# A hybrid encoder step in fp32: weight sums of the channel stage by accumulating DMAs, and smaller state-space edits

## The chip, the cores and the metric

The kernel runs as one program on 1 core of one Trainium2 chip. The metric is device time in microseconds (us), the median of 3 runs. Six things work side by side in a core: TensorE (PE) multiplies, its weight loads (PEld) run beside the products, VectorE (DVE) and ScalarE (ACT) do elementwise work, GpSimd (POOL) and SyncE (SP) issue transfers, and DMA engines move the data. Each engine executes its own queue in order; semaphores connect them.

## The reference, cut to what matters

One layer is applied to 512 prompt rows and 128 sample rows (8 x 16), 640 in all. The mixing sub-layer comes first, the channel sub-layer behind it:

```
def encoder_layer(x, c, ...):
    u = rms_norm(x, g_pre_mix) * (1 + sc1) + sh1          # sc1, sh1 from silu(c) @ w_ada
    proj = u @ w_in                                       # -> z, xbc, dt_raw, p, gates
    ...                                                   # conv over xbc -> xs, bm, cm
    dt = softplus(dt_raw + dt_bias)
    y, h_final = ssd_chunked(xs, dt, a, bm, cm, h0)       # decay = exp(min(a_cs_l - a_cs_s, causal))
    y = y + xs * d_skip
    ...                                                   # norm, w_ssd_out, pooling branch, gates, w_o
    x = x + gt1 * rms_norm(mix, g_post_mix)
    v = rms_norm(x, g_pre_mlp) * (1 + sc2) + sh2
    hdn = jnp.square(jax.nn.relu(v @ w_up))               # 1024 -> 4096
    x = x + gt2 * rms_norm(hdn @ w_down, g_post_mlp)      # 4096 -> 1024
```

## The kernel before

**Precision.** Most products of fp32 data are made of three products of a reduced type: a matrix is split into a high half (ACT casts it) and a low half (DVE subtracts the cast from the original), and PE makes high x high, high x low and low x high. `split` (L132, L133) does this for weights: `wh`/`wl` are rings of four buffers, and every fifth split goes to the one buffer `wxh`/`wxl`.

**Prologue.** `ada_cols` makes the normalized input `uu` of two of eight row blocks and splits it; `dt_part` (L390 to L396) multiplies the dt weights with both halves in plain fp32 products, 80 instructions in all. `wpl`, the weight of the pooling branch, is loaded into room that the prologue's tiles leave.

**State space.** Eight groups, five blocks of 128 rows each: 40 calls of `common`. It reads the running sum `acs` back as rows (`ab`), subtracts each row's own sum by adding `nacs` and clips at zero in four DVE instructions (L711), takes one exponential on ACT (L712) and multiplies by `cb` (L713). `skip` (L720) adds D times x to the output from PSUM `py` in two DVE instructions a block.

**Channel sub-layer.** The 4096 hidden columns are cut in eight chunks e of 512. Each chunk has an up stage, two pairs (e,0) and (e,1) of 256 columns, and a down stage (`down`, L1219 for the products `pd`, L1237 for the sums into `acc`), which runs one chunk behind. A pair cuts its 1024 x 256 weight tile `wu` into four blocks (i,j), i the column half and j the row half, and its rows v in halves likewise; seven block products replace eight (84 instructions of 320 columns). For that it needs sums of weight blocks, made in the one buffer `S` by four DVE additions of 128 x 512:

```
first():   z = (2,1) + (2,2)        L1146       x0 = split of columns 0:128
           s = z + (1,1)            L1147       x1 = split of the two sums
second():  S[1] = s + (1,2)         L1154       x2 = split of the two sums
           S[0] = (1,1) + (2,1)     L1155       x3 = split of (2,2)
```

`run` makes the products (L1168): `pq` is a bank pair with the parts A_ and B_, `pr` the bank C_. The parts are emptied into `p1`, `u2`, `u3`, `q5` and the hidden tiles `f1`, `f2`; `put_hid` splits these (L1086, L1087). `t_blocks` makes the sums of v (t1 to t4, split into `TH`, `TL` and `AH`) from a copy of v which `make_v` wrote to DRAM (`v_d`, ten writes of 256 KB on POOL's queue). Chunk 0 is made without blocks before, beside the end of the mixing sub-layer; then come t_blocks, the down stage of chunk 0, and the pairs from (1,0) on. The next pair's `load` and `first` run inside `run` of the one ahead or inside `down`, at the row block t = 3.

**Order.** A scheduler sets each engine's order from the program's order and priorities; the high-priority parts are the splits and the sums. All loads of this stage are on SP's queue; POOL issues nothing there.

## Time and profile before

| what | value |
|---|---|
| median of 3 runs | 1381.33 us (1377.14 to 1384.82) |
| the profiled execution, its time | 1377.68 us |
| its span in the trace | 1375.9 us |
| PE busy | 1331.1 us (97%) |
| DVE busy | 918.0 us (67%) |
| ACT busy | 538.6 us (39%) |
| POOL busy | 90.8 us (7%) |
| DMA, mean | 140 GB/s |

How to read it: busy time is what an engine executes, and the span is the profiled execution from its first instruction to its last. An engine at 97% leaves little idle time to remove; the others wait for it. The stages lie about so: prologue to 90 us, input projection and state space to 627, the mixing output and v to 960, chunks 1 to 7 from 985 to the end.

### The profile page before, as it was taken

What the parts mean: (1) busy time and instruction counts of PE and PEld (TensorE: products, weight loads), DVE (VectorE), ACT (ScalarE), POOL (GpSimd) and SP (SyncE); (2) the same over time, 40 slices, a digit from 0 to 9 for tenths busy, and PEclk for the clock granted to TensorE, in tenths of its full rate; (3) what the DMA queues carried; (4) which work ended last, traced back from release to release, by engine and by line L of the source; (5) the groups of instructions that cost most, each with busy time, mean ns of one, the idle gap of its engine ahead of it and who ended that gap; (6) DMA issues with size and microseconds to landing.
All of it is one profiled execution on the core that took longest, in us unless ns stands there. A gap on an engine that the chain in (4) does not pass through costs nothing.

```text
span 1375.9 us, 22421 instructions
## 1 busy us (share of the span) xinstructions
PE 1331.1 (97%) x9008; PEld 1194.5 (87%) x9008; DVE 918.0 (67%) x1900; ACT 538.6 (39%) x961; POOL 90.8 (7%) x153
## 2 busy tenths in 40 slices
PE   4999999999999999999998999999989999999997
PEld 3999998878888889889898999788888988888886
DVE  4775668777776879687557332587575856757675
ACT  4443435444434454553434221355442422423331
POOL 0010010101201020102100000011000000000000
PEclk9999999999999999999999999999999999999999
DMA  9743523565546553435368533645122302122151
GB/s 295 224 102 119 167 88 111 154 218 184 164 149 219 179 181 87 131 104 172 111 206 268 193 111 119 214 153 184 32 82 72 123 31 92 67 88 92 62 199 46
DMA packets 134928, 192.26 MB, mean 140 GB/s; under 512 B 8541, under 2 KB 104877, under 8 KB 132776
## 3 DMA queue, kind: packets, MB, share of 16 engines
q1 hardware_dynamic: 124808, 161.27, 36.8%
q0 software_dynamic: 10016, 29.56, 6.9%
q8 instruction: 71, 1.16, 0.4%
q14 instruction: 33, 0.27, 0.1%
HBM read 159.20 MB, written 31.60 MB: 139 GB/s over the span
## 4 chain that ended last, share of the span: by engine, by line
PE 84%; DVE 5%; issue 4%; DMA 4%; ACT 2%; SPq 0%; POOL 0%; DVEq 0%; ACTq 0%; POOLq 0%
PE pd L1219 16%; PE px L161 16%; PE pz L161 8%; PE pso L161 8%; PE pq L1168 8%; PE pga L161 4%; PE pr L1168 3%; PE pp L161 3%; PE po L984 3%; PE py L725 2%; PE sp L745 1%; PE hTp L778 1%; PE ada L300 1%; PE yo L783 1%; PE tp L698 1%
## 5 line engine op out<-in xcount | busy, mean ns | idle before, releaser
L161 PE MATMUL px<-AH,wh 128*128 128x256 f32 (+1 forms) x512 | 119.1, 314 | 0.0
L161 PE MATMUL px<-AH,wl 128*128 128x256 f32 (+1 forms) x512 | 118.5, 310 | 0.0
L161 PE MATMUL px<-AL,wh 128*128 128x256 f32 (+1 forms) x512 | 118.0, 310 | 0.0
L161 PEld LDWEIGHTS px<-AH,wh 128*128 128x128 f32 x512 | 91.5, 188 | 7.8 <-issue 4.4
L161 PEld LDWEIGHTS px<-AL,wh 128*128 128x128 f32 x512 | 93.2, 188 | 0.5 <-issue 0.5
L161 PEld LDWEIGHTS px<-AH,wl 128*128 128x128 f32 x512 | 93.1, 188 | 0.5 <-issue 0.5
L1237 DVE TENSOR_TENSOR acc<-acc,pd 128x512 f32<-128x512 f32 (+1 forms) x61 | 41.1, 676 | 75.2 <-PE pd L1219 75.1
L1219 PE MATMUL pd<-wh,hh 128*128 128x512 f32 (+1 forms) x223 | 87.2, 394 | 1.9 <-ACT wh L132 1.7
L1219 PE MATMUL pd<-wl,hh 128*128 128x512 f32 (+1 forms) x223 | 87.9, 394 | 0.6 <-DVE wl L133 0.6
L1219 PE MATMUL pd<-wh,hl 128*128 128x512 f32 (+1 forms) x223 | 87.2, 393 | 0.0
L638 DVE SCALAR_TENSOR_TENSOR ac<-rw,colw,ac 128x640 f32<-128x640 f32 x96 | 84.4, 879 | 1.2 <-ACT ac L636 0.9
L161 PE MATMUL pz<-AH,wh 128*128 128x256 f32 (+1 forms) x256 | 62.1, 318 | 0.0
L161 PE MATMUL pz<-AH,wl 128*128 128x256 f32 (+1 forms) x256 | 61.6, 316 | 0.0
L161 PE MATMUL pz<-AL,wh 128*128 128x256 f32 (+1 forms) x256 | 61.5, 316 | 0.0
L161 PE MATMUL pso<-ynh,wh 128*128 128x256 f32 (+1 forms) x256 | 58.4, 309 | 2.6 <-ACT tgb L587 2.6
L132 ACT CAST wh<-S 128x1024 fp32r<-128x1024 f32 x22 | 23.1, 1048 | 95.2 <-DVE acc L1237 39.4
L161 PE MATMUL pso<-ynl,wh 128*128 128x256 f32 (+1 forms) x256 | 58.3, 309 | 0.0
L161 PE MATMUL pso<-ynh,wl 128*128 128x256 f32 (+1 forms) x256 | 58.2, 309 | 0.0
L1219 PEld LDWEIGHTS pd<-wh,hh 128*128 128x128 f32 x223 | 41.7, 188 | 12.6 <-ACT wh L132 2.7
L161 PEld LDWEIGHTS pz<-AH,wh 128*128 128x128 f32 x256 | 45.7, 188 | 6.1 <-issue 4.3
L1219 PEld LDWEIGHTS pd<-wl,hh 128*128 128x128 f32 x223 | 41.9, 188 | 10.2 <-DVE wl L133 1.5
L1219 PEld LDWEIGHTS pd<-wh,hl 128*128 128x128 f32 x223 | 41.9, 188 | 9.7 <-DVE hl L1087 0.3
(483 smaller groups left out, 3677.5 us busy)
## 6 DMA issues: line engine op xcount, KB each, us to landing
wada<-in_w_ada_dram SPq DMA_DIRECT2D x24, 1024.0 KB
wu<-in_w_up_dram SPq DMA_DIRECT2D x16, 1024.0 KB
wd<-in_w_down_dram SPq DMA_DIRECT2D x16, 1024.0 KB
ab<-acs_d SPq DMA_DIRECT2D x40, 256.0 KB
wxs<-in_w_in_dram SPq DMA_DIRECT2D x8, 1024.0 KB
wbc<-in_w_in_dram SPq DMA_DIRECT2D x16, 512.0 KB
wz<-in_w_in_dram SPq DMA_DIRECT2D x8, 1024.0 KB
h<-in_state_ssm_dram SPq DMA_DIRECT2D x16, 512.0 KB
```

Source lines behind the costliest of these rows:

```text
L132: S.copy(h, src)
L161: T.matmul(reg(ps, g), ww[:, kw, :], aa[g][:, ka, :], start=first and i == 0 and j == 0, stop=last and i == n - 1 and j == 2)
L300: T.matmul(st["ps"][32 * cg:32 * cg + 32, 0:n], cT[:, k, :], st["w"][:, k % kr, n * cg:n * (cg + 1)], start=k == 0, stop=k == 7, tile_posi ...
L638: V.scalar_tensor_tensor(a3, rw[:, :, k:k + 16], colw[:, 32 * k + ci:32 * k + ci + 1], a3, ALU.mult, ALU.add)
L698: T.transpose(tp[:, 128 * i:128 * (i + 1)], xc[:, i, ts], ident)
L725: T.matmul(py[64 * j:64 * (j + 1), 128 * qq:128 * (qq + 1)], xr[:, 2 * qq + j, :], M[:, 2 * qq + j, :], start=True, stop=stop)
L745: T.matmul(sp[:, 0:256], bt, xrd, start=True, stop=True)
L778: T.transpose(pt[:, 128 * b:128 * (b + 1)], st["h0"][qq][:, 4 * hb + b, :], ident)
L984: T.matmul(ps[:, HC[half]], aa[:, k, :], ww[:, HC[half]], start=k == 0 and j == 0, stop=k == 7 and j == 2)
L1168: T.matmul(dst, ww[:, k, :], aa[:, k, :], start=start and k == 0 and j == 0, stop=stop and k == 3 and j == 2, skip_group_check=True)
L1219: T.matmul(ps, aa[:, k, :], ww[:, cols], start=first and k == 0 and j == 0, stop=last and k == n - 1 and j == 2)
L1237: V.tensor_tensor(acc[t][:, hc], acc[t][:, hc], ps, ALU.add)
```

## The change

It has five parts.

1. `dt_part` multiplies the dt weights with `uu` itself instead of its two halves: 40 instructions instead of 80. The tile `uu` is kept in `uus`.
2. In `common` the clip is made first, in one DVE instruction on 128 x 512: min(ab, pacs), where `pacs` is the running sum with its own sign. Then four ACT instructions take the exponential with `nacs` as bias. D times x is written into `yb` by two ACT copies per group (`start`), and `skip` is one DVE addition of 128 x 256 per block.
3. `t_blocks` loads v into `acc_f` and works in place; the split of t3 is given back as `t3_late`. Pair (1,0) is made without block sums (`plain`, 96 products), ahead of t3's split; pair (1,1) follows, then the down stage of chunk 0, then chunks 2 to 7 as before. `run` uses `f1` and `f2` in place of `u2`, `u3`, `q5`.
4. Of the four sums of a pair, DVE makes one: z1 = s0 + (1,2) (L1164 in the changed kernel), at high priority.
5. The other three are made by DMAs into two buffers `Sa` and `Sb`, one of each. For Sa, SP loads block (2,1) into both halves; POOL adds (2,2) to both and then (1,1) to s0. For Sb, SP loads (1,1) into z0 and POOL adds (2,1). `sums_a` of the next pair is issued behind this pair's `first`, `sums_b` behind its `second`.

The diff, cut to these parts:

```diff
     def dt_part(b, k):
-        for j, aa in enumerate((uh, ul)):
-            for t in range(4):
-                T.matmul(dps[32 * t:32 * t + 32, 0:128], wdt[:, k, :], tok_cols(aa, t)[:, k, :].bitcast(F32),
-                         start=k == 0 and j == 0, stop=k == 7 and j == 1, tile_position=(0, 32 * t))
-            T.matmul(dps4[32 * b:32 * b + 32, 0:128], wdt[:, k, :], tok_cols(aa, 4)[:, k, :].bitcast(F32),
-                     start=k == 2 * b and j == 0, stop=k == 2 * b + 1 and j == 1, tile_position=(0, 32 * b))
+        uu = uus[b]
+        for t in range(4):
+            T.matmul(dps[32 * t:32 * t + 32, 0:128], wdt[:, k, :], uu[:, k - 2 * b, 128 * t:128 * (t + 1)],
+                     start=k == 0, stop=k == 7, tile_position=(0, 32 * t))
+        T.matmul(dps4[32 * b:32 * b + 32, 0:128], wdt[:, k, :], uu[:, k - 2 * b, 512:640],
+                 start=k == 2 * b, stop=k == 2 * b + 1, tile_position=(0, 32 * b))
...
         S.activation(nacs, acs_ps, AF.Copy, scale=-1.0)
+        S.copy(pacs, acs_ps)
...
+            V.tensor_tensor(M, ab, pacs[:, t, hs].unsqueeze(2).broadcast_to([128, 4, 128]), ALU.min)
             for hh in range(4):
-                V.tensor_scalar(M[:, hh, :], ab[:, hh, :], nacs[:, t, 4 * g + hh:4 * g + hh + 1], 0.0, ALU.add, ALU.min)
-            S.activation(M, M, AF.Exp)
+                S.activation(M[:, hh, :], M[:, hh, :], AF.Exp, bias=nacs[:, t, 4 * g + hh:4 * g + hh + 1])
...
-        def skip(qq, ts, py):
-            V.scalar_tensor_tensor(st["yb"][:, qq, ts], st["xc"][:, qq, ts], dsk[:, 2 * g + qq:2 * g + qq + 1],
-                                   py[:, 128 * qq:128 * (qq + 1)], ALU.mult, ALU.add)
+        def skip(ts, py):
+            yt = st["yb"][:, :, ts]
+            V.tensor_tensor(yt, yt, py[:, 0:256].rearrange("p (q n) -> p q n", q=2), ALU.add)
 
...
         def start():
+            for qq in range(2):
+                S.activation(st["yb"][:, qq, :], st["xc"][:, qq, :], AF.Copy, scale=dsk[:, 2 * g + qq:2 * g + qq + 1])
...
     def t_blocks():
-        vs = [F.tile([128, 4, 640], F32R, tag="h" + c, name=f"vs{c}", bufs=2).bitcast(F32) for c in "hl"]
-        for i, v in enumerate(vs):
-            Y.dma_start(v, v_d[4 * i:4 * i + 4].rearrange("k p n -> p k n"))
-        f11, f12, f21, f22 = vs[0][:, :, 0:HT], vs[0][:, :, HT:640], vs[1][:, :, 0:HT], vs[1][:, :, HT:640]
-        c1, c2, c3 = (acc_f[:, 1280 * i:1280 * (i + 1)].rearrange("p (k n) -> p k n", k=4) for i in (1, 2, 3))
+        vs = acc_f.rearrange("p (k n) -> p k n", k=8)
+        for i in range(2):
+            Y.dma_start(vs[:, 4 * i:4 * i + 4], v_d[4 * i:4 * i + 4].rearrange("k p n -> p k n"))
+        f11, f12, f21, f22 = vs[:, 0:4, 0:HT], vs[:, 0:4, HT:640], vs[:, 4:8, 0:HT], vs[:, 4:8, HT:640]
 
         def st(dst, src):
             S.copy(dst[0], src)
             V.tensor_tensor(dst[1], src, dst[0].bitcast(F32), ALU.subtract)
 
-        V.tensor_tensor(c1, f11, f12, ALU.subtract)
-        V.scalar_tensor_tensor(c2, c1, -1.0, f22, ALU.mult, ALU.subtract)
-        st(t1, c1)
-        st(t2, c2)
-        V.scalar_tensor_tensor(c3, c2, -1.0, f21, ALU.mult, ALU.subtract)
-        st(t4, c3)
-        V.tensor_tensor(c1, f22, f12, ALU.subtract)
-        st(t3, c1)
+        V.tensor_tensor(f11, f11, f12, ALU.subtract)
+        V.tensor_tensor(f12, f22, f12, ALU.subtract)
+        V.scalar_tensor_tensor(f22, f11, -1.0, f22, ALU.mult, ALU.subtract)
+        st(t1, f11)
+        st(t2, f22)
+        V.scalar_tensor_tensor(f21, f22, -1.0, f21, ALU.mult, ALU.subtract)
+        st(t4, f21)
+        return lambda: st(t3, f12)
 
...
+        def sums_a(self):
+            self.s = s = Q.tile([128, 2, 4, 128], F32, tag="Sa", name=f"Sa{self.n}", bufs=1)
+            Y.dma_start(s[:, 0], self.src(2, 1))
+            Y.dma_start(s[:, 1], self.src(2, 1))
+            G.dma_start(s[:, 0], self.src(2, 2), accum_op=ALU.add)
+            G.dma_start(s[:, 1], self.src(2, 2), accum_op=ALU.add)
+            G.dma_start(s[:, 0], self.src(1, 1), accum_op=ALU.add)
+
+        def sums_b(self):
+            self.z = z = Q.tile([128, 2, 4, 128], F32, tag="Sb", name=f"Sb{self.n}", bufs=1)
+            Y.dma_start(z[:, 0], self.src(1, 1))
+            G.dma_start(z[:, 0], self.src(2, 1), accum_op=ALU.add)
+
...
         def first(self):
-            r = self.r
-            self.s = sm = Q.tile([128, 2, 4, 128], F32, tag="S", name=f"S{self.n}", bufs=1)
+            self.x0 = split(self.r[:, :, 0:128], *KF)
             with tc.high_priority():
-                V.tensor_tensor(sm[:, 1], self.blk(2, 1), self.blk(2, 2), ALU.add)
-                V.tensor_tensor(sm[:, 0], sm[:, 1], self.blk(1, 1), ALU.add)
-            self.x0 = split(r[:, :, 0:128], *KF)
-            self.x1 = split(sm, *KH)
+                V.tensor_tensor(self.z[:, 1], self.s[:, 0], self.blk(1, 2), ALU.add)
+            self.x1 = split(self.s, *KH)
 
         def second(self):
-            sm = self.s
-            with tc.high_priority():
-                V.tensor_tensor(sm[:, 1], sm[:, 0], self.blk(1, 2), ALU.add)
-                V.tensor_tensor(sm[:, 0], self.blk(1, 1), self.blk(2, 1), ALU.add)
-            self.x2 = split(sm, *KH)
+            self.x2 = split(self.z, *KH)
             self.x3 = split(self.blk(2, 2), "p (k f) -> p k f", dict(k=4), n=512)
+
...
+        def plain(self):
+            for i in range(2):
+                ps = big(f"pq{self.n}{i}")
+                w = split_k(self.r, i)
+                for k in range(8):
+                    for j, (ww, aa) in enumerate(((w[0], vh), (w[0], vl), (w[1], vh))):
+                        for g in range(2):
+                            T.matmul(ps[:, 512 * g:512 * g + HT], ww[:, k, :], aa[g][:, k, :], start=k == 0 and j == 0, stop=k == 7 and j == 2)
+                f = rl_tile(self.e, 2 * self.fp + i)
+                for g in range(2):
+                    S.activation(f[:, HT * g:HT * (g + 1)], ps[:, 512 * g:512 * g + HT], AF.Relu)
+                V.tensor_tensor(f, f, f, ALU.mult)
+                put_hid(self.e, 2 * self.fp + i, f)
 
...
-            p1, u2, u3, q5 = tl("p1"), tl("u2"), tl("u3"), tl("q5")
+            p1 = tl("p1")
             f1, f2 = rl_tile(e, 2 * self.fp), rl_tile(e, 2 * self.fp + 1)
             prod(A_, a11, b11, True, True)
             S.copy(p1, A_)
             prod(B_, sl(self.x1, 0), t2, True, True)
-            V.tensor_tensor(u2, p1, B_, ALU.add)
+            V.tensor_tensor(f1[:, HT:640], p1, B_, ALU.add)
             prod(C_, sl(self.x1, 1), t1, True, True)
-            S.copy(q5, C_)
+            S.copy(f2[:, 0:HT], C_)
             if nxt:
                 nxt()
             prod(A_, a12, b21, False, True)
             S.copy(f1[:, 0:HT], A_)
             prod(B_, sl(self.x2, 0), t3, False, True)
-            V.tensor_tensor(u3, p1, B_, ALU.add)
+            V.tensor_tensor(f2[:, HT:640], p1, B_, ALU.add)
+            V.tensor_tensor(f2[:, HT:640], f2[:, HT:640], f2[:, 0:HT], ALU.add)
             prod(C_, sl(self.x2, 1), b22, False, True)
-            V.tensor_tensor(f1[:, HT:640], u2, C_, ALU.add)
+            V.tensor_tensor(f1[:, HT:640], f1[:, HT:640], C_, ALU.add)
             V.scalar_tensor_tensor(f1, f1, 0.0, f1, ALU.max, ALU.mult)
             put_hid(e, 2 * self.fp, f1)
             prod(B_, self.x3, t4, False, True)
-            V.tensor_tensor(f2[:, HT:640], u3, q5, ALU.add)
             V.tensor_tensor(f2[:, 0:HT], p1, B_, ALU.add)
...
     def begin(p):
-        p.load()
         p.first()
-
-    def up(e, after, late):
+        if NX[p]:
+            NX[p].sums_a()
+
+    def run(p, after, late):
+        p.second()
+        if NX[p]:
+            NX[p].sums_b()
+        p.run(nxt=after, late=late)
+
+    up0()
+    hid[1] = hid_tiles(1)
+    P[0].load()
+    t3_late = t_blocks()
+    P[1].sums_a()
+    P[1].sums_b()
+    P[0].plain()
+    t3_late()
+    P[1].load()
+    begin(P[1])
+    w = []
+    run(P[1], lambda: w_rows(0, [], 0, w), lambda: w_rows(0, [], 1, w))
+    P[2].load()
+    down((0,), [w], nxt=lambda: begin(P[2]))
+    for e in range(2, 8):
+        w = []
         hid[e] = hid_tiles(e)
         pa, pb = pairs[e, 0], pairs[e, 1]
-        pa.second()
-        pa.run(nxt=lambda: begin(pb), late=pb.second)
-        pb.run(nxt=after, late=late)
-
-    up0()
-    w0 = w_rows(0, [], 1, w_rows(0, [], 0, []))
-    t_blocks()
-    down((0,), [w0], nxt=lambda: begin(pairs[1, 0]))
-    up(1, lambda: begin(pairs[2, 0]), None)
-    for e in range(2, 8):
-        w = []
-        up(e, lambda: w_rows(e - 1, [], 0, w), lambda: w_rows(e - 1, [], 1, w))
+        pb.load()
+        run(pa, lambda: begin(pb), None)
+        run(pb, lambda: w_rows(e - 1, [], 0, w), lambda: w_rows(e - 1, [], 1, w))
         if e < 7:
-            down((e - 1,), [w], nxt=lambda: begin(pairs[e + 1, 0]))
+            pc = pairs[e + 1, 0]
+            pc.load()
+            down((e - 1,), [w], nxt=lambda: begin(pc))
```

The order of the instructions shows three places. The first is DVE between the weights of chunk 0 and the down stage, where t1, t2 and t4 are split (L1119 before, L1121 now; TL is the tile of their low halves) and pair (1,1) gets its sums. Before:

```order
L1122 SCALAR_TENSOR_TENSOR acc_10227<-acc_10227,vsl_10280 128x1280
L1087 TENSOR_TENSOR hl0_10234<-rl03_10253,hh0_10233 128x640
L1119 TENSOR_TENSOR TL_10232<-acc_10227,TH_10231 128x1280 x2
L1125 SCALAR_TENSOR_TENSOR acc_10227<-acc_10227,vsl_10280 128x1280
L1127 TENSOR_TENSOR acc_10227<-vsl_10280,vsh_10279 128x1280
L1119 TENSOR_TENSOR TL_10232<-acc_10227,TH_10231 128x1280
```

And now:

```order
L1121 TENSOR_TENSOR TL_10170<-acc_10165,TH_10169 128x1280
L1164 TENSOR_TENSOR Sb11_10219<-Sa11_10213,wu11_10342 128x512
L133 TENSOR_TENSOR wxl_10350<-Sa11_10213,wxh_10349 128x1024
L1090 TENSOR_TENSOR hl0_10172<-rl03_10191,hh0_10171 128x640
L133 TENSOR_TENSOR wl_10360<-Sb11_10219,wh_10359 128x1024
L133 TENSOR_TENSOR wl_10364<-wu11_10342,wh_10363 128x512
L1121 TENSOR_TENSOR TL_10170<-acc_10165,TH_10169 128x1280
```

The sum of pair (1,1) and the splits that use it stand between the splits of t1 and t2.

The second is the start of chunk 3, on DVE: pair (3,1) gets its weights while pair (3,0) runs. The names carry the pair's number; `u330`, `rl30` and `rl31` empty the banks of pair (3,0). Before:

```order
L1146 TENSOR_TENSOR S31_11189<-wu31_11187 128x512
L1147 TENSOR_TENSOR S31_11189<-S31_11189,wu31_11187 128x512
L133 TENSOR_TENSOR wl_11197<-S31_11189,wh_11196 128x1024
L1192 TENSOR_TENSOR u330_11144<-p130_11142,pq30_11140 128x320
L1154 TENSOR_TENSOR S31_11189<-S31_11189,wu31_11187 128x512
L1194 TENSOR_TENSOR rl30_11146<-u230_11143,pr30_11141 128x320
L1155 TENSOR_TENSOR S31_11189<-wu31_11187 128x512
```

And now:

```order
L1210 TENSOR_TENSOR rl30_11092<-p130_11091,pq30_11089 128x320
L1164 TENSOR_TENSOR Sb31_11086<-Sa31_11012,wu31_11076 128x512
L133 TENSOR_TENSOR wl_11139<-Sa31_11012,wh_11138 128x1024
L133 TENSOR_TENSOR wxl_11208<-Sb31_11086,wxh_11207 128x1024
L133 TENSOR_TENSOR wl_11212<-wu31_11076,wh_11211 128x512
L1218 TENSOR_TENSOR rl31_11093<-p130_11091,pq30_11089 128x320
L1221 TENSOR_TENSOR rl30_11092<-rl30_11092,pr30_11090 128x320
```

The one sum that is left stands at the head of the three splits of pair (3,1), and L1218, which reads pair (3,0)'s bank `pq30`, stands behind them. On PE at the same place pair (3,0)'s last product (`pq30` with TH and TL) and pair (3,1)'s first two (`pq31`, `pr31`) follow each other. Before:

```order
L1168 MATMUL pq30_11140<-TH_10231,wh_11136 128x320
L1168 MATMUL pq30_11140<-TL_10232,wh_11136 128x320
L1168 MATMUL pq30_11140<-TH_10231,wl_11137 128x320
L1168 MATMUL pq31_11269<-AL_76,wxh_11192 128x320
L1168 MATMUL pq31_11269<-AH_75,wxl_11193 128x320
L1168 MATMUL pq31_11269<-AH_75,wxh_11192 128x320
```

And now:

```order
L1194 MATMUL pq31_11218<-AH_75,wh_11133 128x320
L1194 MATMUL pq31_11218<-AL_76,wh_11133 128x320
L1194 MATMUL pq31_11218<-AH_75,wl_11134 128x320
L1194 MATMUL pr31_11219<-TH_10169,wh_11138 128x320
L1194 MATMUL pr31_11219<-TL_10170,wh_11138 128x320
L1194 MATMUL pr31_11219<-TH_10169,wl_11139 128x320
L1194 MATMUL pr31_11219<-TH_10169,wh_11138 128x320
L1194 MATMUL pq30_11089<-TH_10169,wh_11082 128x320
```

Pair (3,0)'s last product now stands behind the whole first product (12) of pair (3,1) and four instructions of its second.

The third is POOL's queue, which ended with the writes of v:

```order
L1037 DMA v_d_86<-vv01_10031 128x4x128
L1037 DMA v_d_86<-vv00_10018 128x4x128
L1037 DMA v_d_86<-vv10_10075 128x4x128
L1037 DMA v_d_86<-vv11_10088 128x4x128
L1313 UNCONDITIONAL_BRANCH
```

Now four accumulating transfers for each of 13 pairs follow; the first pair's and the next one's read:

```order
L1040 DMA v_d_86<-vv11_10026 128x4x128
L1149 DMA Sa11_10213<-in_w_up_dram 128x4x128
L1150 DMA Sa11_10213<-in_w_up_dram 128x4x128
L1156 DMA Sb11_10219<-in_w_up_dram 128x4x128
L1151 DMA Sa11_10213<-in_w_up_dram 128x4x128
L1149 DMA Sa20_10353<-in_w_up_dram 128x4x128
```

The second addition to s0 (L1151) stands behind that to z0 (L1156).

## Rows read from the trace of the kernel before

**Rows 1.** The page, first part: busy time, share of the span, instructions.
```profile
span 1375.9 us, 22421 instructions
PE 1331.1 (97%) x9008; PEld 1194.5 (87%) x9008; DVE 918.0 (67%) x1900; ACT 538.6 (39%) x961; POOL 90.8 (7%) x153
```

**Rows 2.** Busy time by windows: stretch, length, each engine, granted clock, DMA share, GB/s.
```profile
200.00:600.00 400.00, 397.27 (x3003) 344.59 (x3002) 310.88 (x754) 183.97 (x354) 46.27 (x76) 1.00 0.52 159
985.00:1043.70 58.70, 55.12 (x349) 51.35 (x348) 46.55 (x66) 26.42 (x39) 0.00 (x0) 1.00 0.27 90
1043.70:1096.00 52.30, 52.30 (x286) 46.31 (x286) 34.33 (x48) 16.27 (x22) 0.00 (x0) 1.00 0.24 81
1043.70:1315.00 271.30, 268.88 (x1441) 234.97 (x1441) 174.48 (x240) 83.58 (x112) 0.00 (x0) 1.00 0.23 78
```

**Rows 3.** The chain of waits, 1060 to 1100 us: start, length, what.
```profile
1059.94 8.37 PE pd L1219 x36
1068.31 1.75 PE pq L1168 x12
```

**Rows 4.** Waits from 980 to 1376 us: us in total, times, longest.
```profile
PEld pr L1168 <- ACT q L1186: 3.2, 8, 0.8
...
PE pd L1219 <- ACT wh L132: 1.7, 3, 0.6
```

**Rows 5.** The chain of waits, 0 to 90 us: shares by line, two pieces.
```profile
by line: PE pp L161 22.9%; PE ada L363 7.0%; DMA wpl<-in_w_pool_group_dram 6.8%; PE uT L406 5.7%; DMA rowf<-in_pool_scale_dram 5.7%; PE dtp L393 5.5%; issue 4.7%; ACT junk L332 3.3%; DVE wl L133 2.5%; PE ypp L161 2.3%; PE dtp L395 2.1%; SPq
...
55.71 0.23 PE dtp L395 x2
...
55.96 6.16 DMA wpl<-in_w_pool_group_dram
```

**Rows 6.** Groups by line, 180 to 627 us: count, busy, mean ns, idle before.
```profile
L711 DVE TENSOR_SCALAR M<-ab,nacs 128x128 f32<-128x128 f32 x140 | 34.9, 293 | 1.9 <-PE py L725 1.9
...
L713 DVE TENSOR_TENSOR M<-M,cb 128x512 f32<-128x512 f32 x35 | 23.9, 684 | 0.0
...
L720 DVE SCALAR_TENSOR_TENSOR yb<-xc,dsk,py 128x128 f32<-128x128 f32 x70 | 23.1, 343 | 9.9 <-PE py L796 4.4 <-PE py L740 2.6 <-PE py L725 2.4
L712 ACT ACTIVATE M<-M 128x512 f32<-128x512 f32 x35 | 22.2, 634 | 49.6 <-DVE M L711 49.6
...
L811 ACT ACTIVATE bm<-hl,cst 128x128 fp32r<-128x128 f32 x56 | 17.8, 390 | 0.5 <-DVE hl L806 0.5
...
L705 ACT COPY bt<-tp 128x128 f32<-128x128 f32 x35 | 9.3, 264 | 24.6 <-DVE xr L703 24.6
...
L752 DVE TENSOR_TENSOR hn<-hn,sp 128x256 f32<-128x256 f32 x21 | 8.7, 416 | 0.1
...
L833 ACT ACTIVATE sr<-sz 128x640 f32<-128x640 f32 x6 | 4.4, 738 | 3.2 <-DVE sz L678 3.1
```

**Rows 7.** Groups by line, 985 to 1376 us, DVE: the block sums.
```profile
L1155 DVE TENSOR_TENSOR S<-wu 128x512 f32<-128x512 f32 x14 | 9.6, 687 | 0.1
...
L1146 DVE TENSOR_TENSOR S<-wu 128x512 f32<-128x512 f32 x13 | 8.9, 686 | 0.3 <-DMA wu<-in_w_up_dram 0.2
```

**Rows 8.** Timeline, 1066 to 1075 us: start, length, instruction, [idle before].
```profile
1066.25 1.05 ACT L132 CAST wh<-S 128x1024 fp32r<-128x1024 f32 x1 [17.51 <-PE pd L1219]
...
1067.33 1.23 DVE L133 TENSOR_TENSOR wl<-S,wh 128x1024 fp32r<-128x1024 f32 x1 [1.09 <-ACT wh L132]
...
1068.15 0.31 PE L1168 MATMUL pq<-AH,wh 128*128 128x320 f32 x1
...
1072.71 0.49 DVE L1184 TENSOR_TENSOR u<-p,pq 128x320 f32<-128x320 f32 x1 [1.23 <-PE pq L1168]
...
1073.12 1.22 DVE L133 TENSOR_TENSOR wl<-S,wh 128x1024 fp32r<-128x1024 f32 x1
...
1074.25 0.68 DVE L133 TENSOR_TENSOR wl<-wu,wh 128x512 fp32r<-128x512 f32 x1
```

**Rows 9.** The chain of waits, 940 to 960 us: a load from issue to use.
```profile
947.74 5.71 DMA wu<-in_w_up_dram
```

**Rows 10.** The page, DMA issues: queue, count, KB each, median us to landing.
```profile
v_d<-vv POOLq DMA_DIRECT2D x10, 256.0 KB, 3.1
```

**Rows 11.** Busy time by windows, as rows 2: v_d writes, then one 1 MB load.
```profile
914.90:916.10 1.20, 1.20 (x7) 0.97 (x6) 1.20 (x11) 0.52 (x1) 0.21 (x1) 1.00 0.81 236
1045.50:1049.30 3.80, 3.80 (x18) 3.08 (x17) 3.54 (x6) 0.73 (x1) 0.00 (x0) 1.00 0.91 276
```

More of the change, by code (lines that the diff above doesn't have):

```diff
@@ L230, in tile_hybrid_step @@
     nacs = cp.tile([128, NT, 32], F32, name="nacs")
+    pacs = cp.tile([128, NT, 32], F32, name="pacs")
     dte = cp.tile([128, NT, 32], F32, name="dte")
@@ L349, in tile_hybrid_step @@
         spT.append(sp_.rearrange("p (i r) -> p i r", r=120))
-    adap = {}
+    adap, uus = {}, {}
     def ada_load(b):
@@ L377, in ada_cols @@
                                colf[:, GPM + 2 * b:GPM + 2 * b + 2].unsqueeze(2).broadcast_to([128, 2, 9]), ALU.add, ALU.mult)
-        uu = pr.tile([128, 2, 640], F32, tag="uu", name=f"uu{b}", bufs=1)
+        uu = uus[b] = pr.tile([128, 2, 640], F32, tag="uu", name=f"uu{b}", bufs=1)
         for i in range(2):
@@ L741, in prompt @@
                                  start=False, stop=True)
-            for qq in range(2):
-                skip(qq, ts, py)
+            skip(ts, py)
             sp = bank("sp" + n)
```

7 lines of the change are left out of this document (6 added, 1 removed).

## The prediction

> **What bounds the kernel now.** I read the page's busy line first, then stretches, then the chain of waits, then single instructions. TensorE (PE) is busy 1331.1 of 1375.9 us [rows 1]; the reader should see how little PE time is left to win. From 200 to 600 us PE is busy 397.27 of 400, while VectorE (DVE) has 310.88 and ScalarE (ACT) 183.97 [rows 2]. From 1043.7 to 1315 us it is busy 268.88 of 271.30. The one loose place is 985 to 1043.7 us: 58.70 us pass for 349 recorded matmuls, against 52.30 us for 286 in the stretch behind it. Twelve 320-column products take 1.75 us on the chain [rows 3], 0.147 us each, and the whole kernel's waits are short: in all of 980 to 1376 us PE's longest sum of waits is 1.7 us and its weight loads' is 3.2 us [rows 4]. So an instruction taken off DVE or ACT pays only where PE waits for it, and a transfer costs only where PE comes to wait for it. Span and launch: the profiled execution took 1377.68 us, 1.78 over its span, and stands 3.65 below the median of 1381.33; I make the sum against 1377.7.
>
> **Part 1, the dt products.** Dropping the low halves removes 40 of 80 instructions. In the chain of waits from 0 to 90 us the dt products stand for 5.5% and 2.1% [rows 5], 7.6% of 90 = 6.8 us; half is 3.4 us. They are on the path: the last of them ends at 55.94, and the load of wpl starts there, whose tile takes the place of the prologue's. What is late next is the other PE work of the stretch, which has no gap. The new reader of uu holds that single buffer a little longer, but the products are also free sooner, since they wait for no split. Bounds 0 and -3.4; I take **-3.0**.
>
> **Part 2, the state-space changes.** Per block (40 blocks) DVE loses four L711 of 293 ns and two L720 of 343 ns, and gains one 512-wide operation (684 ns as L713) and one 256-wide one from PSUM (about 416 ns as L752): 1172 + 686 - 684 - 416 = 0.76 us, 30 us in all. ACT loses one L712 of 634 ns and gains four 128-wide ones, each between 264 ns (L705) and 390 ns (L811), so +0.42 to +0.93 us per block, and two 128x640 copies per group at about 0.74 us (L833, 16 of them): 29 to 49 us [rows 6]. Both lie beside a PE that idles 2.73 us in 400 [rows 2]. A gain is bounded by that, a loss by the same order if an exponential comes late. I take **0**, bounds -3 and +3.
>
> **Part 3, another order of chunks.** Pair (1,0) is now made plainly while the blocks t1 to t4 are built, and the first down products go behind pair (1,1). The plain pair has 96 products in place of 84: 12 x 0.147 = **+1.8**. The loose stretch would be freed: 349 matmuls, some 14 of them 512 wide at 8.37 / 36 = 0.23 [rows 3], are 51.3 + 1.2 = 52.5 us, so 6.2 us are lost there now; I take **-5**, and **-2** for the scattered waits later [rows 4]. Against that, DVE meets the z sum of pair (1,1) ahead of the low half of t2; its chain of DMAs starts behind the 2.5 MB of v and can make PE wait between 0 and 4 us: **+1.5**. Together -3.7, bounds -7 and +1.
>
> **Part 4, the DVE sums that go.** Three of four 0.69 us sums (L1146, L1147, L1154, L1155) go in 13 pairs, 27 us of DVE [rows 7]. In the steady stretch PE waits for none of them: **0**.
>
> **Part 5, the DMA sums that come.** This decides. Every pair from (1,1) has three loads on SP's queue and four accumulations on POOL's. For the second pair of an up stage (six times, e = 2 to 7) they are on a short leash. Let R be the first product of pair (e,0), 1068.15 in the trace [rows 8].
>
> Start: Sa has one buffer, free once pair (e,0)'s x1 is split. That split ends at 1067.33 + 1.23, R + 0.4. POOL issues in the order s0, s1, z0, s0 again; the last must have seen the first land.
>
> Need: DVE's queue, in the order after, holds for pair (e,1): the z sum, which waits for the last accumulation, then the low halves of x1, x2 and x3, and only then L1218, which empties the bank that pair (e,0)'s last product writes. From landing: ACT's cast 1.05, x1's low half 1.23, x2's 1.22, x3's 0.68, L1218 0.49 (as L1184) and some 0.2 of hand-overs make 4.9 us [rows 8]. PE comes to that product after 72 + 12 + 4 = 88 products, R + 12.9. So the chain must land by **R + 8.0**. Queued behind the waiting z sum are all further DVE steps of the stage, and behind the waiting cast on ACT the casts of x2, x3 and the hidden tiles; PE waits for both.
>
> Length: no row of before shows an accumulation. Load leg: 5.71 us from issue to use for 1 MB [rows 9], less three quarters of the 3.8 us that the packets of 1 MB take at 276 GB/s [rows 11]: 2.9 us. Accumulation leg, lower end: v_d, the same 256 KB in the same 512-byte runs on the same queue, lands 3.1 us after issue [rows 10]; its movement takes about 1.1 us, 256 KB at the 236 GB/s of a stretch in which such writes ran [rows 11]. Then it lands at 0.4 + 2.9 + 3.1 + 3.1 = R + 9.5, a wait of 1.5 us. Upper end: if each accumulation moves its data twice, once to read what is there, and all four run one behind the other with the 1 MB of wd (3.8 us) in their midst, then 0.4 + 2.9 + 2.0 + 4 x 2.2 + 3.8 = R + 17.9, a wait of 9.9 us. With movement doubled alone the legs are 4.2 us: R + 11.7. I take R + 12, the doubled legs with 0.3 us of queueing, because the destination has to be read in any case: a wait of **4 us, six times, +24**. PE has nothing else in its queue, since its order is fixed.
>
> By the Trainium skill, "Collectives: The Full Stack", section "The bandwidth ceiling: the fold count and why AG != RS != AR", an add in the DMA engines needs two source reads and so runs at half the rate of a copy; no run here shows it yet, and by it the estimate would be R + 11.7, 3.7 us a time.
>
> **Sum.** 1377.7 - 3.0 + 0 - 3.7 + 0 + 24 = **1395 us**, slower by about 1%.
>
> **Rivals.**
>
> A. *The chain fits* (the other side of zero). Place: the same six waits. If a leg takes 2.9 us or less, the chain lands by R + 9.1, the waits sum to under 6.7 us, and the -6.7 us of parts 1 and 3 win; from 2.4 us a leg nothing waits: 1371. At v_d's 3.1 us the six waits cost 9 us: 1380, no change to be measured. For it: v_d's row, and engines with room (DMA share 0.23 in 1043.7 to 1315 [rows 2]). Against it: v_d does not read its destination. From 2.4 to 2.9 us a leg it gives 1371 to 1378; I put it at 1374, and at 1371 and below where parts 1 and 3 bring more than I took (their bounds sum to -10.4). By the Trainium skill, "DMA: Bandwidth & Descriptors", section "Anatomy of one DMA — SWDGE (gpsimd) path", a DMA of this queue takes 2.0 us and its bytes at 436 GB/s, an estimate of 2.6 us here. By it the six waits would cost 3 us and this rival would hold; v_d's 3.1 us stands half a microsecond above it.
>
> B. *The accumulations queue up.* Their packets share the engines with wd and with each other, R + 17.9: 9.9 us, six times, +59: 1430. For it: POOL issues s1 and z0 ahead of the second addition to s0, and SP issues wd behind z's load at the same moment. Against it: a 1 MB load is over in 3.8 us.
>
> C. *The sums do not matter, the stages do.* That the change does not do what it says: the state-space part turns PE's 2.73 us of idle time in 400 into more, because ACT makes four exponentials in a row ahead of the casts that feed PE. Price: 0.5 us per block at the most that reaches PE, 40 x 0.5 = 20 us, without any wait in the last stage: 1391. Against it: ACT is busy 46% there.
>
> **How the numbers follow.** Forecast 0.55 (its own range 1385 to 1408), A 0.27, B 0.13, C 0.05. The range takes in A from 1371 and B's near half: **1371 to 1422**. A measurement of this kernel can tell about 0.5% (7 us) from no change. Slower by more: the forecast without its lower edge 0.47, B 0.13, C 0.02, together 0.62; within: that edge 0.08, A with legs near 3 us 0.08, C 0.03, together 0.19; faster by more: the rest of A, legs short of that with the gains of parts 1 and 3 in their larger half, 0.19. Measured against the median of 1381.33, the forecast would stand 3.65 higher, which the range holds.
>
> **What would show it.** In the trace after, each up stage from e = 2 should have one hole in PE of about 4 us, ahead of the first pair's last product or the second pair's first pr product, put down to DVE or ACT, and behind it ACT's cast of Sa waiting for a POOL DMA. The POOL rows of Sa should land 4 us or more after issue. No hole and a landing near 3 us is rival A; a hole of 9 us is B. The stretch that was 985 to 1043.7 us should hold less idle PE. The dt products should take half, and the work after them start some 3 us sooner; if the state-space stage as a whole changes by more than 3 us, part 2 was wrong. The forecast fails most easily on one number, the time of an accumulation, which I took without a row for it.

## The result

The changed kernel takes 1441.99 us (median of 4 runs, 1439.8 to 1448.36) against 1380.22 us before. The ratio is 1.0457, with a 95% interval from 1.0433 to 1.0481: slower by 4.6%. The forecast was 1395 us and a range up to 1422, so the direction was right and the size was not: some 62 us slower where 17 had been forecast.

### The profile page after: what moved, and what is told of

Read it like the earlier page. It is cut to its first block, busy times and chain, and to the rows that moved or that the text cites. A ratio compares the mean times of both kernels' runs of the same rounds, so it can differ in the third digit from the quotient of the medians.

```text
span 1442.4 us, 22449 instructions
## 1 busy us (share of the span) xinstructions
PE 1350.0 (94%) x8940; PEld 1213.5 (84%) x8940; DVE 870.2 (60%) x1690; ACT 571.4 (40%) x1097; POOL 157.9 (11%) x205
## 3 DMA queue, kind: packets, MB, share of 16 engines
q0 software_dynamic: 37472, 43.19, 14.1%
## 4 chain that ended last, share of the span: by engine, by line
PE 34%; DMA 9%; issue 5%; DVE 4%; ACT 2%; POOL 1%; DVEq 0%; SPq 0%; ACTq 0%; POOLq 0%
PE pd L1245 14%; PE pso L161 8%; DMA Sa<-in_w_up_dram 7%; PE pq L1194 4%; PE po L987 3%; DVE wl L133 2%; PE pr L1194 1%; PE pga L161 1%; DMA wu<-in_w_up_dram 1%; ACT wh L132 1%; DMA bf_d<-ypl 1%; PE pgb L161 1%; PE pu03g L167 0%; PE pu L167 0%; DMA wo<-in_w_o_dram 0%
## 5 line engine op out<-in xcount | busy, mean ns | idle before, releaser
L714 ACT ACTIVATE M<-M,nacs 128x128 f32<-128x128 f32 x160 | 52.4, 396 | 17.6 <-DVE M L712 17.6
L132 ACT CAST wh<-Sa 128x1024 fp32r<-128x1024 f32 x10 | 10.5, 1048 | 121.6 <-PE pd L1245 77.5
L1164 DVE TENSOR_TENSOR Sb<-Sa,wu 128x512 f32<-128x512 f32 x13 | 9.0, 691 | 79.7 <-DMA Sa<-in_w_up_dram 75.2
L1245 PEld LDWEIGHTS pd<-wl,hh 128*128 128x128 f32 x223 | 41.9, 188 | 12.9 <-DVE wl L133 3.8
```

Source lines behind the costliest of these rows:

```text
L132: S.copy(h, src)
L714: S.activation(M[:, hh, :], M[:, hh, :], AF.Exp, bias=nacs[:, t, 4 * g + hh:4 * g + hh + 1])
L1164: V.tensor_tensor(self.z[:, 1], self.s[:, 0], self.blk(1, 2), ALU.add)
L1245: T.matmul(ps, aa[:, k, :], ww[:, cols], start=first and k == 0 and j == 0, stop=last and k == n - 1 and j == 2)
```

## The profile after

The page's busy line, to be held against [rows 1]:

```profile
span 1442.4 us, 22449 instructions
...
PE 1350.0 (94%) x8940; PEld 1213.5 (84%) x8940; DVE 870.2 (60%) x1690; ACT 571.4 (40%) x1097; POOL 157.9 (11%) x205
```

The span grew by 66.5 us. PE has fewer matmuls, yet is busy 18.9 us longer, and idles 92.4 us instead of 44.8. Both halves of that need an explanation. Busy time by windows says where (stretch, length, busy time of each engine, granted clock, DMA share, GB/s, as in [rows 2]):

```profile
180.00:627.00 447.00, 442.57 (x3360) 388.56 (x3359) 331.00 (x694) 237.44 (x518) 53.74 (x88) 1.00 0.49 153
960.00:1440.00 480.00, 424.94 (x2161) 370.45 (x2159) 244.37 (x371) 132.64 (x193) 65.59 (x51) 0.93 0.52 122
```

Up to the channel sub-layer little happens: PE idles 4.4 us in the 447 of the projection and the state space. Behind them, at 743 us, it stands once for 5.9 us (waiting for ACT), where the kernel before had two idle times of 2.2 and 2.6 us. Behind 960 us it idles 55 us, and the mean granted clock is 0.93. The waits of that stretch from 985 us on (waiting engine and line, what it waits for, us in total, times, longest) name one cause; no such row stood in [rows 4]:

```profile
DVE Sb L1164 <- DMA Sa<-in_w_up_dram: 71.3, 7, 12.4
...
PE pr L1194 <- ACT wh L132: 24.4, 5, 5.6
...
PE pq L1194 <- DVE rl L1218: 7.4, 6, 1.2
```

DVE stands at the one sum that is left, z1 (L1164), for the last accumulation into Sa; ACT stands at the cast of Sa; PE waits for that cast, and then for L1218, which DVE has behind z1 and three low halves. That is the hole which the prediction had described. One of the six, in chunk 3, as the chain of waits shows it (start, length, what):

```profile
1090.22 7.55 DMA Sa<-in_w_up_dram
1097.77 0.28 issue
1098.05 4.90 DMA Sa<-in_w_up_dram
1102.95 0.02 issue
1102.97 1.05 ACT wh L132
1104.03 0.02 issue
1104.05 1.24 DVE wl L133
```

And its instructions in the timeline (start, length, engine, line, operation, idle time before and its releaser in brackets):

```profile
1086.60 0.37 SPq L1147 DMA_DIRECT2D Sa<-in_w_up_dram  x1
...
1088.54 0.37 SPq L115 DMA_DIRECT2D wd<-in_w_down_dram  x1
...
1104.07 0.63 PE L1194 MATMUL pr<-TH,wh 128*128 128x320 f32 x1 [5.05 <-ACT wh L132]
...
1105.33 0.63 PE L1194 MATMUL pr<-TH,wl 128*128 128x320 f32 x1 [0.36 <-DVE wl L133]
...
1107.46 0.63 PE L1194 MATMUL pq<-TH,wh 128*128 128x320 f32 x1 [1.23 <-DVE rl L1218]
```

The first product of pair (3,0) is at 1086.17, the R of the prediction. The loads of Sa are issued at R + 0.4; by the trace's semaphore events the first has landed at R + 3.4, and POOL issues the first accumulation 0.7 us later, at R + 4.1. The second addition to s0 is issued at R + 11.9 and has landed at R + 16.8. PE comes to pair (3,0)'s last product at 1107.46, R + 21.3, where 88 products of 0.147 us would have brought it at R + 12.9: 8.4 us late, of which 5.05 + 0.36 + 1.23 = 6.6 us is idle. (In the six chunks the sum lands between R + 15.8 and R + 17.3, and PE is 7.5 to 9.0 us late.) The other 1.8 us show in the windows around and behind the hole; the third is the part of the second in which the clock is low:

```profile
1098.60:1104.00 5.40, 0.42 (x3) 0.16 (x2) 0.69 (x1) 1.03 (x2) 0.72 (x1) 0.76 0.58 71
1104.00:1114.00 10.00, 8.34 (x34) 7.45 (x35) 7.83 (x11) 4.31 (x7) 3.88 (x3) 0.62 0.73 200
1104.00:1111.60 7.60, 5.94 (x19) 5.14 (x20) 5.43 (x9) 3.01 (x5) 2.85 (x3) 0.50 0.62 189
```

While PE stands, the granted clock falls to 0.50 of full speed, the level of 1.2 GHz, and stays there for 7.6 us behind the hole. In that time the products come every 0.27 us instead of every 0.147 us. So a hole is paid twice, idle first and then slow.

## The experiments

**One: the sums by DVE again.** Is it the DMA sums at all, or the new order and the state-space edits?

```diff
-    sums_a, sums_b: loads and accumulations into Sa, Sb
+    first():  Sa[1] = (2,1) + (2,2); Sa[0] = Sa[1] + (1,1)      on DVE
+    second(): Sb[1] = Sa[0] + (1,2); Sb[0] = (1,1) + (2,1)      on DVE
```

> The changed kernel with all four block sums of a pair made by DVE again (in Sa and Sb), nothing by accumulating DMAs; order of chunks, plain pair, dt and state-space parts as in the changed kernel. My theory: the DMA sums alone cost the time (six holes of 4.1 to 5.6 us and two short waits behind each, and the half clock that follows each), the rest of the change brings a few us. It expects 1372 to 1380 us, PE idle after 960 us under 8 us in all, granted clock 1.00 throughout. Rival: the new order and the plain pair cost a good part themselves: 1390 us or more, with holes left at other places. Second rival: the first idle stretch at 743 us belongs to the state-space part and stays, which would show as 1380 or more with no hole after 960.

Measured: 1373.78 us, ratio 0.9954 [0.9939, 0.9968] against the kernel before. It is the fastest kernel of this study, half a percent faster than before.

```profile
span 1372.8 us, 22282 instructions
...
PE 1328.5 (97%) x8940; PEld 1196.8 (87%) x8940; DVE 893.3 (65%) x1729; ACT 569.9 (42%) x1097; POOL 90.7 (7%) x153
```

The DMA sums alone cost the time, 69.6 us of span. This page also divides it: the same 8940 recorded matmuls are busy 1328.5 us here and 1350.0 there, 21.5 us for the half clock, and the other 48.1 us are idle. The rival of holes left elsewhere is out; behind 960 us PE meets two idle times over half a microsecond, 1.45 and 0.54 us. The second rival is out too: the idle time near 743 us stays (4.7 us here, 6.6 us in experiment four), and both kernels take no longer than the one before. One thing changes besides the DMAs: z1 is made in `second` again, and so stands elsewhere in DVE's order; experiments five and nine bear on that.

**Two: the same transfers without adding.** Is it the addition, or that transfers follow each other?

```diff
-            G.dma_start(s[:, 0], self.src(2, 2), accum_op=ALU.add)
+            G.dma_start(s[:, 0], self.src(2, 2))          # likewise the other three
```

> The changed kernel with the same transfers on the same queues in the same order, but those of POOL write instead of adding, so that the block sums hold no sums (the additions are left out). Theory one, an accumulating packet's own length decides (512-byte packets took 65 ns where those of plain loads took 27): 2048 packets on 16 engines take 3.5 us instead of 8.3 us, the last transfer lands some 4.8 us earlier, the hole of about 6.6 us a stage falls under 2 us and the clock stays at 1.00: 1385 to 1400 us. Theory two, the waits between the transfers and the queue's start-up decide (two dependent legs behind a load): the landing moves by under 2 us, the holes stay above 4 us: 1425 us or more.

Measured: 1423.35 us, ratio 1.0304 [1.0279, 1.0329]; the block sums are left out here. It falls between the two theories and nearer to the second. The software queue's share of the 16 DMA engines, on the page's part 3 (packets, MB, share), before, after and in this run:

```profile
q0 software_dynamic: 10016, 29.56, 6.9%
```

```profile
q0 software_dynamic: 37472, 43.19, 14.1%
```

```profile
q0 software_dynamic: 14176, 43.19, 9.7%
```

After: 14.1% of 1442.4 less 6.9% of 1375.9 is 108 us, 8.3 us for each of 13 pairs, or 65 ns for a 512-byte packet (26,624 of them). A plain load's 512-byte packet takes 27 ns in the same trace. Without adding it is 9.7% of 1421.1 less 94.9, 43 us, 3.3 us a pair, in 4096-byte packets. The packet size changed along with the adding, but it is not what costs: 43 us on 16 engines are 206 ns for each of 3,328 packets, 26 ns for 512 bytes, as in the plain load's small packets. Adding thus takes 2.4 to 2.5 times as long for the same data. By the Trainium skill, "Collectives: The Full Stack", section "The bandwidth ceiling: the fold count and why AG != RS != AR", the add of a collective's reduce step reads two sources and runs at half the rate of a copy; the 2.4 here, of additions within one core, agrees in direction and lies above it. But the landing moved by less than half of what theory one asked: from the first transfer's issue to the sum's landing it is 10.5 us instead of 12.7. The timeline of POOL in this run:

```profile
1082.59 0.75 POOL L1149 DMA_DIRECT2D Sa<-in_w_up_dram  x1 [37.63 <-DVE acc L1263]
...
1089.83 0.75 POOL L1151 DMA_DIRECT2D Sa<-in_w_up_dram  x1 [3.57 <-DMA Sa<-in_w_up_dram]
```

(The brackets name the latest event before an instruction, here DVE's `acc`; what the first transfer waits for is its load, whose landing it follows by the same 0.57 us in every second pair of this run.) The first leg, from s0's first transfer to its second, takes 7.2 us even as a copy (7.8 as an addition), the second one 3.3 us (4.9). The last leg got shorter by 1.6 us and the first by 0.6. Something else stretches the first.

**Three: 36 products of no use per pair.** This was to fill the hole and so to price the clock.

```diff
             S.copy(p1, A_)
+            if self.fp:
+                with tc.high_priority():
+                    for _ in range(3):
+                        prod(C_, a11, b11, True, True)
             prod(B_, sl(self.x1, 0), t2, True, True)
```

> The changed kernel with 36 products of no use (320 columns, into the bank pr ahead of its first real product) in each of the seven pairs (1,1) to (7,1); they are ready as soon as the pair's first weights are split and give the chain of DMAs 5.3 us more. If a hole costs its idle time and nothing else, the products take the place of idle time and the total stays at 1442 or rises. If a hole also costs the clock (granted 0.50 for some 10 us at each hole), the clock stays at 1.00 with the holes shorter than 2 us, and the total falls by 12 to 20 us to 1422 to 1430 though PE has 252 instructions more.

Measured: 1466.9 us, ratio 1.0631 [1.0615, 1.0647]. It fails as a test: the products ran early in pair (e,0), but the order on DVE changed with them, z1 now stood ahead of another instruction that pair (e,0) needs, and the holes were longer (5.9 to 7.3 us instead of 4.1 to 5.6). What it shows is only that the blockade moves with DVE's order:

```profile
PE pq L1194 <- DVE rl L1214: 40.8, 7, 7.3
```

**Four: the dt products and the state-space edits alone, on the kernel before.**

```diff
 kernel before
+    parts 1 and 2 of the change, and nothing of parts 3 to 5
```

> The kernel before with the dt products on uu and the state-space edits (parts 1 and 2 of the prediction) alone. By the prediction -3.0 us: 1377. By the two traces, in which the input projection starts 0.4 us later and the state space ends at the same time, 0: within 1378 to 1382, the dt products' time hidden behind the load that follows. Rival C: four exponentials in a row delay the casts: 1390 or more.

Measured: 1378.36 us, ratio 0.999 [0.9978, 1.0003]: no difference that can be told. The state-space rival is out. The 3 us that I had given the dt products are not: they lie at the edge of the interval (-3.0 to +0.4 us), and what speaks against them is the load in the traces, told below. Between this run and the first stands the new order of chunks: 1378.1 to 1372.8 us of span.

**Five: wd's load on POOL's queue.** Is it wd's 1 MB, which SP issues 1.7 us ahead of the first addition, that stretches the leg?

```diff
-                Y.dma_start(v, src)                 # wd
+                G.dma_start(v, src)
```

> The changed kernel with the loads of wd issued on POOL's queue, behind the pair's four accumulating transfers, instead of on SP's behind the load of Sb; nothing is left out. Theory one, the first accumulation (7.5 us from its issue to the second's) is stretched by the 1 MB of wd that moves in its midst: that leg falls to 5.5 us or less, the sum lands 2 us earlier or more, the hole ahead of the first pr product falls from 5 us to 3 us or less: 1415 to 1430 us. Theory two, POOL's own transfers (s0, s1, z0, 8.3 us of packets on 16 engines) fill the leg: it changes by under 0.7 us and the total stays within 1436 to 1446.

Measured: 1421.91 us, ratio 1.0297 [1.0265, 1.033]. The time is within theory one's range, but not for its reason. The load stood ahead of the pair's four additions in POOL's order, not behind:

```profile
1083.55 0.72 POOL L115 DMA_DIRECT2D wd<-in_w_down_dram  x1 [31.26 <-DVE wl L133]
1085.15 1.27 POOL L1149 DMA_DIRECT2D Sa<-in_w_up_dram  x1 [0.88 <-DMA Sa<-in_w_up_dram]
...
1093.08 1.26 POOL L1151 DMA_DIRECT2D Sa<-in_w_up_dram  x1 [4.08 <-DMA Sa<-in_w_up_dram]
```

The leg is 7.9 us, no shorter, and the sum lands at R + 17.0, no sooner (R is 1081.11 here). So this run does not decide about wd. What changed is the order on DVE:

```profile
1091.13 0.49 DVE L1218 TENSOR_TENSOR rl<-p,pq 128x320 f32<-128x320 f32 x1 [4.98 <-PE pq L1194]
...
1098.17 0.69 DVE L1164 TENSOR_TENSOR Sb<-Sa,wu 128x512 f32<-128x512 f32 x1 [5.44 <-DMA Sa<-in_w_up_dram]
```

L1218 now stands ahead of z1, so PE gets through pair (3,0)'s last product without waiting for the chain and then stands at the pr product, for 3.6 us. With the chain as late as before, the total is 20 us lower: as far as these rows show, where the waiting instruction stands in DVE's order is a good part of the price.

**Six: two buffers for Sa.** Is it that the chain starts late?

```diff
-            self.s = s = Q.tile([128, 2, 4, 128], F32, tag="Sa", name=f"Sa{self.n}", bufs=1)
+            self.s = s = Q.tile([128, 2, 4, 128], F32, tag="Sa", name=f"Sa{self.n}", bufs=2)
...
-                V.tensor_tensor(self.z[:, 1], self.s[:, 0], self.blk(1, 2), ALU.add)
+                V.tensor_tensor(self.blk(1, 2), self.s[:, 0], self.blk(1, 2), ALU.add)
```

> The changed kernel with two buffers for Sa, so that the loads and the accumulations of a pair can start a pair earlier; to make room z1 is made in place in the pair's own weight tile and x2 is split in two halves (0.3 us more on ACT and on DVE a pair). All additions remain. Theory one, the late start alone makes the chain miss (it can't begin before the one buffer is free): the wait of z1 and of the cast for Sa goes, what may be left is a wait for Sb's single accumulation of up to 4 us: 1375 to 1405 us. Theory two, the traffic of the accumulations itself costs (it slows wu's and wd's loads or the engines): holes at the same place of over 4 us, 1425 us or more.

Measured: 1428.7 us, ratio 1.0351 [1.0333, 1.0369], outside theory one's range and inside theory two's. Yet the waits for Sa are down to one before the second chunk, and the holes (2.7 to 7.2 us) have moved to the single addition of Sb:

```profile
ACT wh L134 <- DMA Sb<-in_w_up_dram: 35.7, 6, 7.6
PE pq L1196 <- ACT rl L1218: 35.6, 8, 7.2
```

One addition of 256 KB, with neighbours on the engines (wd, s0 and s1 of the next pair), lands 7.1 us behind its issue, again too late, and ACT queues what PE needs behind its cast. The start and the wait had only changed their tile.

**Seven: a hole without transfers.** Does the half clock come from the idle PE, or from the DMA traffic?

```diff
 the kernel of experiment one
-                V.tensor_tensor(s[:, 1], self.blk(2, 1), self.blk(2, 2), ALU.add)
+                for _ in range(15 if self.fp else 1):
+                    V.tensor_tensor(s[:, 1], self.blk(2, 1), self.blk(2, 2), ALU.add)
```

> The kernel of the first experiment (all sums by DVE, no accumulating transfers) with the first sum repeated 14 more times in the pairs (1,1) to (7,1), 9.6 us of DVE each, so that PE meets a hole there without any transfer. If an idle PE is what brings the granted clock to 0.50, the clock falls behind each hole as it did in the changed kernel, PE's busy time rises by 2 to 3 us a hole over the 1328.5 us of the first experiment with the same matmuls, and the total is 1374 plus 6 to 10 us for each of seven holes: 1415 to 1445 us. If the half clock came with the accumulating transfers, the clock stays at 1.00, PE's busy time stays at 1328 to 1331 us, and only the idle time is added.

Measured: 1426.84 us, ratio 1.0338 [1.032, 1.0356], with holes of 4.9 to 6.2 us. Its busy line and two windows, the hole of chunk 2 and what follows it:

```profile
PE 1345.1 (94%) x8940; PEld 1213.8 (85%) x8940; DVE 953.1 (67%) x1827; ACT 570.9 (40%) x1097; POOL 90.8 (6%) x153
```

```profile
1033.40:1039.60 6.20, 0.00 (x0) 0.00 (x0) 6.16 (x10) 2.59 (x5) 0.00 (x0) 0.66 0.00 0
1039.60:1045.00 5.40, 5.38 (x19) 5.19 (x20) 3.69 (x5) 1.44 (x2) 0.00 (x0) 0.50 0.19 41
```

No transfer runs in that hole, and the clock falls all the same. PE's busy time rises by 16.6 us over experiment one with the same matmuls, about 2.4 us for each of seven holes. The price of the clock belongs to the idle PE, whatever made it idle. By the Trainium skill, "TensorE: Matmul & The Clock Gate", section "What's actually happening", PE's default state is throttled and activity releases it; the rows agree, with a mean of 0.66 in the hole and 0.50 behind it.

**Eight: wd's load held back.** The question of experiment five, put so that the order can't escape it: one column of Sa is copied into wd's tile, so that the load waits until s0 has landed.

```diff
+        if gate is not None:
+            V.tensor_copy(r[:, 0:1], gate)          # gate = pb.s[:, 0, 0, 0:1]
         if isinstance(src, (list, tuple)):
```

> The changed kernel with the first wd load of each chunk held until the second pair's sum s0 has landed (a copy of one column by DVE, right behind z1, into the tile that the load fills); order on DVE otherwise as in the changed kernel. In the fifth experiment the load moved from SP to POOL but went ahead of the additions, so it still shared the engines with them. Theory one, wd's 1 MB stretches the first accumulation: its 7.5 us fall to 5.5 or less, s0 lands 2 us earlier or more, the hole ahead of the first pr product falls from about 5 us to 3 or less; total 1410 to 1428 us if the late wd makes no wait of its own (else a new wait ahead of the first pd product). Theory two, POOL's own transfers fill that leg: it stays above 6.8 us and the hole above 4.3.

Measured: 1425.22 us, ratio 1.0347 [1.0329, 1.0366]. POOL in chunk 3:

```profile
1085.26 1.27 POOL L1151 DMA_DIRECT2D Sa<-in_w_up_dram  x1 [36.77 <-DVE acc L1265]
1086.24 1.59 POOL L1152 DMA_DIRECT2D Sa<-in_w_up_dram  x1
1087.32 1.82 POOL L1158 DMA_DIRECT2D Sb<-in_w_up_dram  x1
1090.01 1.27 POOL L1153 DMA_DIRECT2D Sa<-in_w_up_dram  x1 [0.88 <-DMA Sa<-in_w_up_dram]
```

The first leg is 4.75 us instead of 7.8 (4.6 to 4.9 in the six chunks instead of 7.0 to 8.7), and PE's first idle time at the pr product falls from 5.05 to 2.7 us. Theory one holds: wd's load stretches the first addition by 3 us. The second leg, now with s1 and z0 ahead of it, takes 5.6 us instead of 4.9, so the sum lands 2.3 us earlier counted from the loads' issue (14.0 instead of 16.4), not 3.

**Nine: both buffers twice.**

```diff
 the kernel of experiment six
-            self.z = z = Q.tile([128, 4, 128], F32, tag="Sb", name=f"Sb{self.n}", bufs=1)
+            self.z = z = Q.tile([128, 4, 128], F32, tag="Sb", name=f"Sb{self.n}", bufs=2)
-            p1 = tl("p1")
+            p1 = ada.rearrange("p a b -> p (a b)")[:, 0:HT]
```

> The kernel of the sixth experiment with a second buffer for Sb too (room for it by putting p1 into a tile of the prologue that is free by then), so that all three transfers' sums can be made a pair ahead. In the sixth the wait for Sa was gone and one for Sb's single addition (7.1 us) took its place. Theory one, the late start alone makes the holes: no hole over 1.5 us in the pairs from (2,0) on, clock at 1.00, 1372 to 1390 us, about the first experiment. Theory two, the traffic holds something else up (wu or wd land late, another hole over 3 us a chunk): 1400 us or more.

Measured: 1395.05 us, ratio 1.0129 [1.0097, 1.016].

```profile
span 1389.3 us, 22493 instructions
...
PE 1334.4 (96%) x8940; PEld 1203.1 (87%) x8940; DVE 871.3 (63%) x1703; ACT 570.8 (41%) x1110; POOL 157.7 (11%) x205
```

With all additions left in, at a median of 7.7 us from issue to landing for those into Sa (7.5 in the changed kernel, both on the page's list of DMA issues), 47 of the 68 us that lie between the changed kernel and experiment one are gone, because the sums are ready a pair ahead. Theory one holds in the main and misses its range by 5 us. Against experiment one 16.5 us of span remain: 5.9 of PE's busy time at the lower clock and 10.6 of idle time, of which 5.8 us stand at pair (1,1), which has no pair with sums ahead of it, and 5.0 in two holes (2.2 and 2.8 us) in chunks 4 and 6 (all of the profiled execution, the fastest of the four). These two are of the second theory's kind, though shorter than it had them. The chain of waits at them:

```profile
1141.69 8.56 DMA wd<-in_w_down_dram
```

```profile
1253.31 9.10 DMA wd<-in_w_down_dram
```

As wd stretches an addition, the additions stretch wd: 8.6 and 9.1 us from issue to use for 1 MB, where [rows 9] had 5.71 for wu. By the semaphore events of the traces the loads of wd between 1017 and 1260 us land 4.7 to 5.6 us after their issue in experiment one and 7.8 to 9.1 us here. In experiment one no cast waits for wd at all.

## Why the prediction was wrong

**Bounds, place and chain: right.** The wait sits where the prediction put it, in the second pair of each up stage, on the named rows: z1 on DVE for the last addition, ACT's cast behind it, PE at the pr product and then at L1218. The start, R + 0.4, was right to a tenth. The need-by was right as well: landing at R + 16.8 and a need at R + 8.0 give 8.8 us, and PE was 8.4 us late. The load landed 2.9 us after its issue, as reckoned. The doubled movement of an addition, taken because its destination has to be read, is borne out by 65 against 27 ns.

**Length of the chain: the step that failed.** I had 2.9 us for the load leg and two legs of about 4.2 us, "the doubled legs with 0.3 us of queueing", and landed at R + 12. Measured in chunk 3: 3.6, 7.8 and 4.9 us. The 0.7 us in the first of these that go by between the load's landing and POOL's issue had no term. The last leg is 0.7 us over the doubled one; z0's addition, which lands 9.2 us after its issue and 1.0 us ahead of the last, is still on the engines beside it. The middle one shares the engines with wd, and experiment eight takes 3 us out of it by moving wd alone; in all the sum lands 2.3 us sooner by that. Of the 4.8 us by which the chain missed, wd is thus about half; some 1.8 us are left for s1 and z0 on the same engines, which no run shows singly. Rival B named just that, and its landing at R + 17.9 was 1.1 us from the truth. I held against it that "a 1 MB load is over in 3.8 us", and gave it 0.13. That argument was no argument: 3.8 us on a leash of 8 is half of it. The prediction counted wd in the upper bound and then left it out of the value, though SP's order in the changed kernel puts the load right behind Sb's.

**The price of a hole: a term that was missing.** By rival B six holes of 9.9 us gave 1430. With the measured 8.4 us they give 1371 + 50 = 1421. The other 21 us of the measured 1442 are: some 12 us of products behind the holes at the lower clock, 4 us of idle time at pair (1,1) (5.65 against 1.45), and 4 us in three short idle times of the down stage (1.2 to 1.8 us). Of the clock the prediction said nothing; every row of before that it read had a granted clock of 1.00, since no hole of this length was there [rows 2]. Experiments one and seven price it at 21.5 us in the changed kernel and 2.4 us for a hole of 5 to 6 us.

**Part 1: wrong by its whole size, as the traces have it.** The last dt product ends at 54.4 instead of 55.9 and the load of wpl is issued 0.8 us earlier, but ACT's cast of it starts at 63.5 us instead of 62.1: the load takes 8.4 us from issue to use instead of 6.2. The same shows in experiments one, four and nine (63.6 to 64.0). What was "late next" was mostly that load's own time. Experiment four's time alone would not exclude the 3 us.

**Part 2: right.** PE idles 4.4 us from 180 to 627, inside the bound of 3 us more than the 2.73 of [rows 2], and experiment four cannot be told from the kernel before. The sum for DVE was too large: it has 14 us less there, not 26 for the 35 blocks of the window. The 140 instructions of L711 overlap, 34.9 us busy [rows 6] where 140 x 293 ns make 41.

**Part 3: right, a little small.** I had -3.7; experiments four and one, which differ in the order of chunks, in `run`'s temporaries and in having two sum buffers instead of one, are 5.3 us of span and 4.6 us of median apart.

**Part 4: right.** DVE has 23.1 us less than in experiment one, and PE waits for none of them there.

Rival A is refuted: it needed legs of 2.9 us or less, and the shortest of the 39 into Sa took 4.3 us, the median 7.5. Its page, "DMA: Bandwidth & Descriptors", section "Anatomy of one DMA — SWDGE (gpsimd) path" of the Trainium skill, gives by its fit an estimate of 2.6 us for such a transfer; even as a copy, in experiment two, none took less than 3.1. Another section of that page of the Trainium skill, "Issuing engines are not separate DMA queues", says that transfers of several issuing engines share the same 16 DMA engines, and experiment eight agrees: with SP's load of wd held back, POOL's first leg falls from 7.8 to 4.75 us.

## What to carry to other kernels

Moving sums from an engine with room to DMAs replaces 0.7 us by a chain of transfers, and what counts most is the chain's start and its neighbours: an earlier start gave back 47 of 68 us, leaving out the adding 19. List every transfer that the changed order puts on the engines in that time and add all of it before taking a value. Give such a chain buffers enough to start a stage ahead, or leave the sum where it is, and look at what stands behind the waiting instruction in its engine's order. And price a stall of PE of several microseconds at more than its length, because the granted clock falls in it and the work behind it runs slow.
